# Second parts of the weight blocks: a negated rounding on ScalarE and an accumulating DMA in place of a subtraction on VectorE

## The chip, the core and the metric

The kernel runs on one core of a Trainium2 chip. The time is that of one execution in microseconds of the device; three runs of the kernel before gave 2616.05 to 2616.59, median 2616.26. The engines named below are TensorE (PE; its weight loads PEld), VectorE (DVE), ScalarE (ACT), GpSimd (POOL) and SyncE (SP), which here only issues loads and stores. Every engine works through its own list of instructions in order; semaphores tie the lists together.

## What is computed

The reference runs two layers over 512 latent tokens and 256 context tokens of 1024 features, all in float32. Each layer has a SwiGLU half-step, a mixer, and a second SwiGLU half-step, with norms that are scaled and shifted by vectors computed from c:

```python
def _swiglu(h, w1, w3, w2):
    return (jax.nn.silu(h @ w1) * (h @ w3)) @ w2

for l in range(DEPTH):
    x = x + 0.5 * mx[2] * _swiglu(_modulate(_rmsnorm(x, norm_g[l, 0]), mx[0], mx[1]), ...)
    hx = _modulate(_rmsnorm(x, norm_g[l, 1]), mx[3], mx[4])
    ox, oy = _mixer(hx, hy, w_in[l], w_out[l], ...)   # pooling, retention, convolution
    x = x + mx[5] * ox
    x = x + 0.5 * mx[8] * _swiglu(_modulate(_rmsnorm(x, norm_g[l, 2]), mx[6], mx[7]), ...)
return _rmsnorm(x, final_g)
```

The context tokens y take the same steps, but for the last ones of the second layer. The output is the latent stream.

## The kernel before

Features lie on the partitions, tokens along the rows: 256 of the context, 512 latent. A float32 product is made of three passes of the rounded type fp32r. Each operand is written as a first part (the value rounded to fp32r) and a second part (what the rounding left), and `mm3` (L153) multiplies first by first (L155), first by second (L156, weights' first part wh) and second by first (L157, weights' second part wl). `split` (L148) makes the parts: a cast on ScalarE (L150) and a subtraction on VectorE (L151). It serves weights and activations alike.

All weights of the products come as 348 blocks of 128 rows, 284 of 1024 columns (512 KB) and 64 of 640 (320 KB), in the order of use that `weight_order` (L489) lists. `weights` (L519) hands out the next block and prepares those after it: it loads the block into a buffer raw by SP's queue (L528), takes buffers wh and wl and splits. There are 6 buffers of raw, 4 each of wh and wl, and the blocks are prepared 3 ahead of their use (LOOKAHEAD; 0 in the first blocks, before `run` sets it). A buffer of wh or wl can be written when TensorE has used the block four before it for the last time; one of raw can be loaded when the split of the block six before it is done.

TensorE's products run in `products` (L535): over 8 tiles k of the features, and at each k over the outputs that are made together. Most of the time those are one or two blocks at a time. At some places four blocks are begun together, first for the context, then for the latent tokens: `convolution` (L752), `keys` (L708), `values` with four blocks along the features (through `project_tokens`, L623), and the first two tiles of a SwiGLU step (`ffn` L568, `up` L547).

Chains through several engines (norm, taps of the convolution, retention, the vectors of the modulation) are generators, which `poll` resumes when a count of TensorE's time passes their due time. The modulation's vectors need w_mod, loaded in tiles wm (L273 and L355, SP) and summed on VectorE into macc (L301, L303). In the start, `run` (L1056) makes the first norm: diag and rstd on TensorE, rstd copied by ScalarE (L1087), a row modrow copied by ScalarE (L283), then ht on VectorE (L474) and h on ScalarE and VectorE (L476, L478, L480). The first product (L155, up) needs the first h.

In the mixer of the first layer the stream x is not held: `load_x` (L206) reads its 12 tiles back from DRAM by SP's queue before the output projection, whose results VectorE adds to x (L1034). The retention's scores sc are masked on VectorE (L935), then used by TensorE for o (L953); ScalarE scales o to y (L967).

Of the kernel before, what the change touches and what calls it, by code (L numbers as in the profile page):

```python
# [9 lines left out]
F32 = mybir.dt.float32  # L10
F32R = mybir.dt.float32r
I32 = mybir.dt.int32
AF = mybir.ActivationFunctionType
# [19 lines left out]
# groups of tokens: stream, first token, number of tokens  # L33
# [3 lines left out]
LOOKAHEAD = 3  # L37


def per_block(n):  # L40
    """Tiles of the output features in a block of w2 for n tiles of hidden features."""
    return 2 if n * P * 2 <= 1024 else 1
# [3 lines left out]
# columns of the packed per-feature parameters  # L46
# [13 lines left out]
# columns of the constants that depend on shapes alone  # L60
# [11 lines left out]
def pad_cols(pad):  # L72
    """Where the two streams' tokens lie in a row with zeros on both sides of each."""
    return {CTX: pad, LAT: LC + 3 * pad}, NT + 4 * pad


class Kernel:
# [12 lines left out]
    # Chains that pass through several engines are generators: each part is emitted when TensorE has  # L90
    # been given enough other work, counted by self.clock in us, since the part before; a negative
    # delay counts from when the part before was due.
# [25 lines left out]
    def drain(self, *tasks):  # L118
        """Emits what is left of these chains."""
# [28 lines left out]
    def split(self, src, hi, lo):  # L148
        """src = hi + lo exactly, each part narrow enough for one pass of TensorE."""
        self.nc.scalar.copy(hi, src)  # L150
        self.nc.vector.tensor_sub(lo, src, hi.bitcast(F32))  # L151
# [8 lines left out]
    def rsqrt(self, src, n, scale, s):  # L160
        """(src * scale + EPS) ** -0.5 by Newton's steps from a guess by the exponent's bits."""
# [15 lines left out]
    def setup(self):  # L177
# [12 lines left out]
        # silu of both conditions: [P, KD, (ctx, lat)]  # L190
# [7 lines left out]
    def x_slots(self, st, n=LX):  # L198
        """The tiles of a stream and where they lie in its rows of DRAM."""
# [8 lines left out]
    def store_x(self, st):  # L208
        """Makes room while the mixer has no need of the stream."""
# [5 lines left out]
    def decays(self):  # L215
        """Per layer: the masks of decays within a chunk, and the weights by position."""
# [9 lines left out]
        # log1p(e) = 2 atanh(e / (2 + e))  # L226
# [11 lines left out]
        # weights of keys by position, and of a whole chunk: [P, l, dir, h]  # L238
# [37 lines left out]
    def mod_direct(self, l, j, half, raws):  # L276
        """Half of an adaLN vector straight on TensorE, where all engines wait for it."""
# [9 lines left out]
    def mod_halfway(self, l, j, half, raws):  # L287
        """The same with VectorE's multiplications."""
# [16 lines left out]
    def mod_fold(self, acc, rows):  # L305
        """Sums over each 32 partitions; what feature 32 b + i gives lies in column b on partition i."""
# [7 lines left out]
    def mod_sums(self, l, j, halves, rows):  # L314
        """The four sums of each feature together, and the bias: a feature per partition."""
# [16 lines left out]
    def mod_turn(self, row):  # L332
        """Two rows of 512 features to columns: [P, feature tile, condition]."""
# [12 lines left out]
    def mod_chunks(self, l, js, pace):  # L346
        """adaLN vectors in the background: VectorE multiplies, TensorE sums over partitions."""
# [15 lines left out]
    def scale(self, l, idx, st, dt):  # L363
        """Norm weight times 1 + scale for the idx-th sublayer."""
# [26 lines left out]
    def square(self, dt, grp, accs):  # L391
        """Adds the squares of a tile of x to the group's sum."""
# [10 lines left out]
    def mean_square(self, grp, accs):  # L403
        """Sums of squares, a token per partition: [P, tiles of tokens]."""
# [7 lines left out]
    def diag(self, r):  # L412
        """Diagonal matrices of 1 / rms."""
# [8 lines left out]
    def rstd(self, grp, dg):  # L422
        """The same on all partitions, in PSUM."""
# [8 lines left out]
    def put(self, tiles, p, k, grp, s):  # L432
        """part() of a tile that may not have a place yet."""
# [12 lines left out]
    def norm(self, l, idx, grp, accs, h):  # L446
        """Starts a group's norm; need() before its use."""
# [835 lines left out]
```

## Time and profile before

| | us |
|---|---|
| median of the runs | 2616.26 |
| span of the profiled execution | 2612.7 |
| TensorE busy (matmuls) | 2580.8 |
| VectorE busy | 1624.4 |
| ScalarE busy | 722.5 |
| GpSimd busy | 0.2 |

The profile shows one execution; its span runs from the first to the last instruction, so it is a little shorter than a run's time. Matmuls are pipelined, so the durations of neighbours overlap; the distance from one start to the next tells the pace. A view of waits names for each idle stretch of an engine the instruction that ended it. Windows give the busy time of each engine in a stretch of the span, with the clock that was granted to TensorE as a share of its full level (1.00 is 2.4 GHz, 0.50 is 1.2 GHz) and the share of time that the DMA engines were busy. For transfers, the time to landing counts from the issue to the completion.

### The profile page before, as it was taken

What the parts mean: (1) busy time and instruction counts of PE and PEld (TensorE: products, weight loads), DVE (VectorE), ACT (ScalarE), POOL (GpSimd) and SP (SyncE); (2) the same over time, 40 slices, a digit from 0 to 9 for tenths busy, and PEclk for the clock granted to TensorE, in tenths of its full rate; (3) what the DMA queues carried; (4) which work ended last, traced back from release to release, by engine and by line L of the source; (5) the groups of instructions that cost most, each with busy time, mean ns of one, the idle gap of its engine ahead of it and who ended that gap; (6) DMA issues with size and microseconds to landing.
All of it is one profiled execution on the core that took longest, in us unless ns stands there. A gap on an engine that the chain in (4) does not pass through costs nothing. (4 is left out here: it accounts for less than half of the span.)

```text
span 2612.7 us, 35462 instructions
## 1 busy us (share of the span) xinstructions
PE 2580.8 (99%) x14434; PEld 2241.5 (86%) x14434; DVE 1624.4 (62%) x3058; ACT 722.5 (28%) x1204; POOL 0.2 (0%) x4
## 2 busy tenths in 40 slices
PE   8999999999999999999999999999999999999998
PEld 4888888888898888888888888888888888888887
DVE  6776685747977777677333863645536697633335
ACT  3212112133334331212212412121223254422223
POOL 0000000000000000000000000000000000000000
PEclk9999999999999999999999999999999999999999
DMA  7343443322232134354211241433212332233331
GB/s 279 115 146 113 145 153 104 113 85 87 85 97 81 57 105 151 96 158 126 72 61 57 85 134 57 136 105 97 81 58 98 97 109 81 74 106 111 96 96 35
DMA packets 88003, 270.82 MB, mean 104 GB/s; under 512 B 10272, under 2 KB 12832, under 8 KB 87840
## 3 DMA queue, kind: packets, MB, share of 16 engines
q1 hardware_dynamic: 84768, 264.36, 32.1%
q10 hardware_dynamic: 3072, 4.20, 0.6%
q8 instruction: 113, 1.85, 0.3%
q14 instruction: 50, 0.41, 0.0%
HBM read 256.98 MB, written 7.34 MB: 101 GB/s over the span
## 5 line engine op out<-in xcount | busy, mean ns | idle before, releaser
L155 PE MATMUL up<-h,wh 128*128 128x512 f32 (+1 forms) x2496 | 852.1, 343 | 3.4 <-ACT h L476 1.7
L156 PE MATMUL up<-h,wh 128*128 128x512 f32 (+1 forms) x2496 | 853.0, 342 | 0.4 <-DVE h L478 0.2
L157 PE MATMUL up<-h,wl 128*128 128x512 f32 (+1 forms) x2496 | 849.9, 342 | 0.1
L150 ACT CAST wh<-raw 128x1024 fp32r<-128x1024 f32 (+1 forms) x348 | 344.0, 993 | 1261.7 <-PE down L156 442.2
L151 DVE TENSOR_TENSOR wl<-raw,wh 128x1024 fp32r<-128x1024 f32 (+1 forms) x348 | 398.2, 1148 | 333.1 <-ACT wh L150 318.2
L155 PEld LDWEIGHTS up<-h,wh 128*128 128x128 f32 x2496 | 472.2, 190 | 59.4 <-ACT h L476 2.0
L156 PEld LDWEIGHTS up<-h,wh 128*128 128x128 f32 x2496 | 473.0, 190 | 55.9 <-DVE h L478 1.0
L157 PEld LDWEIGHTS up<-h,wl 128*128 128x128 f32 x2496 | 472.3, 189 | 54.5 <-DVE wl L151 0.3
L155 PE MATMUL down<-g,wh 128*128 128x512 f32 (+1 forms) x1264 | 430.9, 341 | 0.0
L156 PE MATMUL down<-g,wh 128*128 128x512 f32 (+1 forms) x1264 | 430.3, 341 | 0.0
L157 PE MATMUL down<-g,wl 128*128 128x512 f32 (+1 forms) x1264 | 429.0, 339 | 0.0
L303 DVE SCALAR_TENSOR_TENSOR macc<-wm,sc,macc 128x512 f32<-128x512 f32 x462 | 319.0, 745 | 9.8 <-DMA wm<-in_w_mod_dram 9.6
L562 DVE TENSOR_TENSOR silu<-silu,up 128x512 f32<-128x512 f32 (+1 forms) x156 | 88.3, 566 | 341.1 <-PE up L157 340.7
L155 PEld LDWEIGHTS down<-g,wh 128*128 128x128 f32 x1264 | 239.7, 190 | 27.5 <-ACT g L150 0.2
L156 PEld LDWEIGHTS down<-g,wh 128*128 128x128 f32 x1264 | 239.8, 190 | 26.8 <-DVE g L151 0.6
L157 PEld LDWEIGHTS down<-g,wl 128*128 128x128 f32 x1264 | 239.3, 189 | 27.1
L599 DVE SCALAR_TENSOR_TENSOR x<-down,gate,x 128x256 f32<-128x256 f32 (+1 forms) x288 | 177.7, 621 | 136.3 <-PE down L157 134.4
L150 ACT CAST g<-silu 128x512 fp32r<-128x512 f32 (+1 forms) x156 | 81.8, 525 | 210.5 <-DVE silu L562 210.5
L745 DVE SCALAR_TENSOR_TENSOR conv<-z,dwh,conv 128x512 f32<-128x512 f32 (+1 forms) x180 | 109.8, 656 | 1.6
L151 DVE TENSOR_TENSOR g<-silu,g 128x512 fp32r<-128x512 f32 (+1 forms) x156 | 88.6, 568 | 23.7 <-ACT g L150 23.6
L561 ACT ACTIVATE silu<-up 128x512 f32<-128x512 f32 (+1 forms) x156 | 77.3, 496 | 87.0 <-PE up L157 86.7
L476 ACT ACTIVATE h<-ht,mod 128x256 fp32r<-128x256 f32 (+1 forms) x96 | 56.3, 597 | 81.5 <-DVE ht L474 81.4
(175 smaller groups left out, 2268.4 us busy)
## 6 DMA issues: line engine op xcount, KB each, us to landing
raw<-in_w_dram SPq DMA_DIRECT2D x224, 512.0 KB, 3.7
wm<-in_w_mod_dram SPq DMA_DIRECT2D x128, 512.0 KB, 3.9
raw<-in_w_dram SPq DMA_DIRECT2D x64, 320.0 KB, 3.0
raw<-in_w_feat_dram SPq DMA_DIRECT2D x36, 512.0 KB, 3.6
wm<-in_w_mod_dram SPq DMA_DIRECT2D x32, 256.0 KB, 6.0
raw<-in_w_out_dram SPq DMA_DIRECT2D x16, 512.0 KB, 4.8
xkept<-x SPq DMA_DIRECT2D x20, 256.0 KB, 2.5
x<-xkept SPq DMA_DIRECT2D x20, 256.0 KB, 6.0
```

What stands on the lines that cost most here:

```text
L150: self.nc.scalar.copy(hi, src)
L151: self.nc.vector.tensor_sub(lo, src, hi.bitcast(F32))
L155: nc.tensor.matmul(out, wh, xh, start=start, stop=False)
L156: nc.tensor.matmul(out, wh, xl, start=False, stop=False)
L157: nc.tensor.matmul(out, wl, xh, start=False, stop=stop)
L303: self.nc.vector.scalar_tensor_tensor(acc[v], raw, s, acc[v], op0=ALU.mult, op1=ALU.add)
L476: nc.scalar.activation(hi, t, AF.Identity, bias=sh)
L561: nc.scalar.activation(t, ps[f, 0], AF.Silu)
L562: nc.vector.tensor_mul(t, t, ps[f, 1])
L599: nc.vector.scalar_tensor_tensor(xd, ps, self.gate(l, idx, grp[0], dt), xd, op0=ALU.mult, op1=ALU.add)
L745: nc.vector.scalar_tensor_tensor(acc, src, w, acc, op0=ALU.mult, op1=ALU.add)
```

## The change

The second part of a weight block is made in another way. ScalarE casts the block into wh as before, and writes the block once more, times −1 and rounded by the same output type, into wl. Then GpSimd issues a DMA from raw to wl that adds what it carries to what lies there: wl = raw − rounded(raw). VectorE has no part in it. There are 5 buffers each of wh and wl and 4 of raw (the same bytes in all), and blocks are prepared 4 ahead. A raw buffer comes free when the accumulate that read it has landed. The rest of the diff takes away comments and texts, and moves line numbers behind L533 by two.

```diff
-LOOKAHEAD = 3
+LOOKAHEAD = 4
...
     def raw(self, n):
-        return self.wpool.tile([P, 1024], F32, tag="raw", name=self.name("raw"), bufs=6)[:, :n]
+        return self.wpool.tile([P, 1024], F32, tag="raw", name=self.name("raw"), bufs=4)[:, :n]
...
             raw = self.raw(n)
             self.nc.sync.dma_start(raw, src)
-            hi = self.wpool.tile([P, 1024], F32R, tag="wh", name=self.name("wh"), bufs=4)[:, :n]
-            lo = self.wpool.tile([P, 1024], F32R, tag="wl", name=self.name("wl"), bufs=4)[:, :n]
-            self.split(raw, hi, lo)
+            hi = self.wpool.tile([P, 1024], F32R, tag="wh", name=self.name("wh"), bufs=5)[:, :n]
+            lo = self.wpool.tile([P, 1024], F32R, tag="wl", name=self.name("wl"), bufs=5)[:, :n]
+            self.nc.scalar.copy(hi, raw)
+            self.nc.scalar.activation(lo, raw, AF.Copy, scale=-1.0)
+            self.nc.gpsimd.dma_start(lo, raw, accum_op=ALU.add)
             self.ahead.append((hi, lo))
```

The order on ScalarE in the start, before: four casts (the first two blocks pairs of the first SwiGLU step), then modrow, rstd and the first tiles of h.

```order
L150 CAST wh_103_347<-raw_102_345 128x1024 [waits DMAHW0_49]
L150 CAST wh_106_353<-raw_105_351 128x1024 [waits DMAHW1_49]
L283 COPY modrow_54_240<-modf_48_196 2x512 [waits PE_49]
L1087 COPY rstd_56_244<-rstd_55_242 128x256 [waits PE_49]
L1087 COPY rstd_58_248<-rstd_57_246 128x512 [waits PE_49]
L476 ACTIVATE h0_83_303<-ht_82_301,mod000_255 128x256 [waits DVE_49]
L476 ACTIVATE h0_83_303<-ht_85_306,mod000_255 128x256 [waits DVE_49]
L476 ACTIVATE h0_87_312<-ht_86_310,mod000_255 128x256 [waits DVE_49]
```

The same place after, from the fourth block's cast on; three pairs of cast and negation stand ahead of these rows.

```order
L531 CAST wh_106_356<-raw_105_354 128x1024 [waits DMAHW1_49]
L532 ACTIVATE wl_107_357<-raw_105_354 128x1024
L283 COPY modrow_54_240<-modf_48_196 2x512 [waits PE_49]
L1089 COPY rstd_56_244<-rstd_55_242 128x256 [waits PE_49]
L1089 COPY rstd_58_248<-rstd_57_246 128x512 [waits PE_49]
L531 CAST wh_109_363<-raw_108_361 128x1024 [waits DMAHW4_49]
L532 ACTIVATE wl_110_364<-raw_108_361 128x1024
L476 ACTIVATE h0_83_305<-ht_82_303,mod000_255 128x256 [waits DVE_49]
L476 ACTIVATE h0_83_305<-ht_85_308,mod000_255 128x256 [waits DVE_49]
```

Each cast is followed by its negation, and a fifth block's pair, which stood behind the tiles of h, stands ahead of the first of them.

The order on SP at the same time, before: loads of raw blocks, two of wm for later vectors, then those of wm0 (L273).

```order
L528 DMA raw_102_345<-in_w13_dram 128x1024 [waits DMAHW0_49]
L528 DMA raw_105_351<-in_w13_dram 128x1024 [waits DMAHW1_49]
L528 DMA raw_108_357<-in_w13_dram 128x1024 [waits DMAHW2_49]
L528 DMA raw_111_363<-in_w13_dram 128x1024 [waits DMAHW3_49]
L355 DMA wm_161_626<-in_w_mod_dram 128x1024 [waits DMAHW4_49]
L355 DMA wm_167_659<-in_w_mod_dram 128x1024 [waits DMAHW5_49]
L528 DMA raw_114_369<-in_w13_dram 128x1024 [waits DMAHW6_49,DVE_49]
L273 DMA wm0_66_269<-in_w_mod_dram 128x512 [waits DMAHW7_49]
```

And after; the names DMASW in a wait are the semaphores of GpSimd's transfers.

```order
L528 DMA raw_102_347<-in_w13_dram 128x1024 [waits DMAHW0_49]
L528 DMA raw_105_354<-in_w13_dram 128x1024 [waits DMAHW1_49]
L355 DMA wm_164_640<-in_w_mod_dram 128x1024 [waits DMAHW2_49]
L355 DMA wm_170_673<-in_w_mod_dram 128x1024 [waits DMAHW3_49]
L528 DMA raw_108_361<-in_w13_dram 128x1024 [waits DMAHW4_49,DMAHW6_49,DMASW0_49,Activation_49]
L528 DMA raw_111_368<-in_w13_dram 128x1024 [waits DMAHW5_49,DMAHW7_49,DMASW1_49,Activation_49]
L273 DMA wm0_66_271<-in_w_mod_dram 128x512
L273 DMA wm0_67_273<-in_w_mod_dram 128x512
```

The fifth and sixth loads of raw have moved behind the two wm, and wait for the transfers that read the first two raw buffers.

The order on TensorE where the keys of the first layer begin, before, up to the first product with the second block's second part (wl_810); the first row is the first product of the keys.

```order
L155 MATMUL kq_877_5630<-h0_766_5097,wh_806_5277 128x256 [waits Activation_49]
L156 MATMUL kq_877_5630<-h1_767_5098,wh_806_5277 128x256
L157 MATMUL kq_877_5630<-h0_766_5097,wl_807_5278 128x256 [waits DVE_49]
L155 MATMUL kq_878_5631<-h0_766_5097,wh_809_5283 128x256 [waits Activation_49]
L156 MATMUL kq_878_5631<-h1_767_5098,wh_809_5283 128x256
L155 MATMUL kq_877_5630<-h0_766_5097,wh_806_5277 128x256
L156 MATMUL kq_877_5630<-h1_767_5098,wh_806_5277 128x256
L155 MATMUL kq_879_5632<-h0_766_5097,wh_812_5289 128x256 [waits Activation_49]
L156 MATMUL kq_879_5632<-h1_767_5098,wh_812_5289 128x256
L157 MATMUL kq_877_5630<-h0_766_5097,wl_807_5278 128x256
L155 MATMUL kq_877_5630<-h0_770_5106,wh_806_5277 128x256
L157 MATMUL kq_878_5631<-h0_766_5097,wl_810_5284 128x256 [waits DVE_49]
```

And after, the last rows up to the same product; 17 matmuls of the keys stand between the convolution's last one and the first of these.

```order
L156 MATMUL kq_880_5720<-h1_778_5201,wh_806_5353 128x256
L157 MATMUL kq_880_5720<-h0_777_5200,wl_807_5354 128x256
L155 MATMUL kq_880_5720<-h0_777_5200,wh_806_5353 128x256
L156 MATMUL kq_880_5720<-h1_778_5201,wh_806_5353 128x256
L157 MATMUL kq_880_5720<-h0_777_5200,wl_807_5354 128x256
L155 MATMUL kq_880_5720<-h0_781_5210,wh_806_5353 128x256
L155 MATMUL kq_883_5723<-h0_769_5179,wh_815_5374 128x256 [waits DVE_49,Activation_49]
L156 MATMUL kq_883_5723<-h1_770_5180,wh_815_5374 128x256
L156 MATMUL kq_880_5720<-h1_782_5211,wh_806_5353 128x256
L157 MATMUL kq_880_5720<-h0_781_5210,wl_807_5354 128x256
L155 MATMUL kq_880_5720<-h0_781_5210,wh_806_5353 128x256
L157 MATMUL kq_881_5721<-h0_769_5179,wl_810_5361 128x256 [waits DMASW5_49]
```

The first product with wl_810 stands 28 matmuls behind the start of the keys, where it stood 11 behind it; products of the first block (kq_880) have moved ahead of it.

The order on SP where x is reloaded, before.

```order
L528 DMA raw_1123_7383<-in_w_out_dram 128x1024 [waits DMAHW0_49,DVE_49]
L528 DMA raw_1190_7873<-in_w_out_dram 128x1024 [waits DMAHW1_49,DVE_49]
L528 DMA raw_1193_7879<-in_w13_dram 128x1024 [waits DMAHW2_49,DVE_49]
L206 DMA x_1102_7341<-xkept_781_5137 128x512 [waits PE_49]
L206 DMA x_1103_7343<-xkept_781_5137 128x512 [waits PE_49]
```

And after: the raw load ahead of the loads of x waits for GpSimd's transfer.

```order
L528 DMA raw_1123_7483<-in_w_out_dram 128x1024 [waits DMAHW2_49,DMAHW6_49,DMASW0_49,Activation_49]
L528 DMA raw_1126_7490<-in_w_out_dram 128x1024 [waits DMAHW3_49,DMASW1_49,Activation_49]
L206 DMA x_1105_7445<-xkept_784_5219 128x512 [waits DVE_49,PE_49]
L206 DMA x_1106_7447<-xkept_784_5219 128x512 [waits DVE_49,PE_49]
L206 DMA x_1107_7449<-xkept_784_5219 128x512 [waits DVE_49]
```

The load of the raw block that stands just ahead of x waited for VectorE (DVE_49), and now for GpSimd's transfer (DMASW1_49).

## Rows read from the trace of the kernel before

**Rows 1.** Page: busy time by engine; then a DMA queue: packets, MB, share.

```profile
PE 2580.8 (99%) x14434; PEld 2241.5 (86%) x14434; DVE 1624.4 (62%) x3058; ACT 722.5 (28%) x1204; POOL 0.2 (0%) x4
...
q1 hardware_dynamic: 84768, 264.36, 32.1%
```

**Rows 2.** TensorE's waits: total us, times, longest us.

```profile
PE cb L862 <- ACT y L967: 1.9, 1, 1.9
...
PE o L953 <- DVE sc L935: 1.6, 2, 1.4
```

**Rows 3.** Windows: busy us by engine (count), granted clock, DMA share, GB/s.

```profile
0.00:60.00 60.00, 47.32 (x171) 22.07 (x171) 40.33 (x90) 21.90 (x38) 0.20 (x4) 0.97 0.82 303
60.00:750.00 690.00, 690.00 (x3951) 608.99 (x3951) 501.80 (x920) 174.97 (x286) 0.00 (x0) 1.00 0.36 112
750.00:850.00 100.00, 95.47 (x615) 84.27 (x614) 68.24 (x241) 46.83 (x114) 0.00 (x0) 0.98 0.29 95
```

**Rows 4.** Page, groups of the splits: total us, mean ns, idle before.

```profile
L150 ACT CAST wh<-raw 128x1024 fp32r<-128x1024 f32 (+1 forms) x348 | 344.0, 993 | 1261.7 <-PE down L156 442.2
L151 DVE TENSOR_TENSOR wl<-raw,wh 128x1024 fp32r<-128x1024 f32 (+1 forms) x348 | 398.2, 1148 | 333.1 <-ACT wh L150 318.2
```

**Rows 5.** Timeline of ScalarE, the start: start us, us, line, operation.

```profile
26.19 1.04 ACT L150 CAST wh<-raw 128x1024 fp32r<-128x1024 f32 x1 [5.60 <-DMA raw<-in_w_dram]
...
30.03 1.05 ACT L150 CAST wh<-raw 128x1024 fp32r<-128x1024 f32 x1 [0.23 <-DMA raw<-in_w_dram]
30.98 0.57 ACT L283 COPY modrow<-modf 2x512 f32<-2x512 f32 x1
31.46 1.03 ACT L1087 COPY rstd<-rstd 128x256 f32<-128x256 f32 x2
32.85 0.91 ACT L476 ACTIVATE h<-ht,mod 128x256 fp32r<-128x256 f32 x2 [0.36 <-DVE ht L474]
```

**Rows 6.** DMA issues: operation, count, KB each, median us to landing.

```profile
swap<-u ACTq DMA_DIRECT2D x64, 64.0 KB, 2.1
```

**Rows 7.** The raw loads' line, L528: landing.

```profile
DMA to landing us min/median/max: 2.8/3.7/9.0
```

**Rows 8.** Timeline of TensorE, the start: the first product.

```profile
33.41 0.50 PE L155 MATMUL up<-h,wh 128*128 128x256 f32 x2 [1.21 <-ACT h L476]
```

**Rows 9.** Windows of 1 us in the first mixer, columns as above.

```profile
795.00:796.00 1.00, 1.00 (x7) 1.00 (x6) 0.00 (x0) 1.00 (x5) 0.00 (x0) 0.50 0.46 168
798.00:799.00 1.00, 1.00 (x7) 0.91 (x6) 0.04 (x1) 1.00 (x4) 0.00 (x0) 0.82 0.00 0
817.00:818.00 1.00, 0.28 (x2) 0.00 (x0) 0.68 (x2) 0.00 (x0) 0.00 (x0) 1.00 1.06 408
```

**Rows 10.** Timeline where the keys begin: TensorE and ScalarE.

```profile
629.67 0.39 PE L157 MATMUL cv<-h,wl 128*128 128x512 f32 x1
...
629.87 2.95 ACT L150 CAST wh<-raw 128x1024 fp32r<-128x1024 f32 x3 [11.47 <-PE cv L156]
629.90 0.39 PE L155 MATMUL cv<-h,wh 128*128 128x512 f32 x1
...
631.94 0.28 PE L155 MATMUL kq<-h,wh 128*128 128x256 f32 x1
...
632.05 0.28 PE L156 MATMUL kq<-h,wh 128*128 128x256 f32 x1
```

**Rows 11.** Timeline at the reload of x, several engines; then its landing, L206.

```profile
804.98 1.22 DVE L151 TENSOR_TENSOR wl<-raw,wh 128x1024 fp32r<-128x1024 f32 x1 [0.76 <-ACT wh L150]
...
806.61 8.14 SPq L206 DMA_DIRECT2D x<-xkept  x12
...
817.32 0.75 DVE L1034 SCALAR_TENSOR_TENSOR x<-mo,mod,x 128x512 f32<-128x512 f32 x1 [3.97 <-PE mo L157]
...
818.73 0.49 PE L953 MATMUL o<-v,sc 128*128 128x128 f32 x2 [1.44 <-DVE sc L935]
...
DMA to landing us min/median/max: 4.3/5.8/6.8
```

## What the change does to the time: the prediction

> **What bounds the kernel now.** I read the busy line of the page first: TensorE's matmuls take 2580.8 of 2612.7 us, VectorE 1624.4, ScalarE 722.5, GpSimd 0.2 [rows 1]. So the end is set by TensorE, and an edit on another engine moves the time only where TensorE waits. The list of what TensorE waited for comes second; past the very start its longest are ScalarE's y (1.9 us) and VectorE's sc (1.6) [rows 2]. No line of that list names the weight blocks' second parts; the splits are early enough everywhere. The windows by stage show where the missing 32 us are: 12.7 in the first 60 us and 4.5 between 750 and 850, while 60 to 750 is full to the last tenth [rows 3]. The rest lies in the second layer's mixer and the tail. What can be won from a free VectorE is therefore some 5 to 10 us, and what can be lost is whatever delay reaches a matmul.
>
> The profiled execution's span is 2612.7 us and the median of the runs 2616.26, 3.6 more; I work on the span and add the same 3.6.
>
> **What the change removes and adds.** 348 subtractions leave VectorE (398.2 us busy), and 348 negative copies come to ScalarE; their nearest row is the cast of the same block, 344.0 us in all and 1.04 us for a block of 1024 columns [rows 4, 5]. ScalarE goes to about 1066 us of 2613: still not the bound as a sum. GpSimd issues 348 accumulating transfers of 320 or 512 KB between two places of SBUF. None is in this trace. Four casts in the start are released 1.28 us apart by the landings of 512 KB blocks, so 1.28 us is what such a block costs all the DMA engines in a stream [rows 5]. If the accumulate reads two operands, it costs twice that: 284 × 2.56 + 64 × 1.6 = 829 us of all engines, 32% of the span on top of the loads' 32.1% [rows 1]. Together 64%: hidden on average.
>
> **How long one accumulate takes (L)**, from issue to landing, is the unknown of this case. Below it: a 64 KB transfer between two places of SBUF lands after 2.1 us [rows 6]. Above it: the slowest raw block took 9.0 us. The nearest row is the median raw block, of the same 512 KB, 3.7 us [rows 7]; the second read adds another 1.28. I take L = 5.0 and keep 2.1 and 9.0 for the range.
>
> The Trainium skill ("DMA: Bandwidth & Descriptors", Anatomy of one DMA) gives 2.0 us plus bytes over 436 GB/s for a GpSimd-issued transfer, 3.2 us for 512 KB; "Collectives: The Full Stack" (Why ReduceScatter is half of AllGather) says that an add in flight is not slow by itself but reads two sources and so runs at half the rate, which makes it 4.4 us, an estimate from these two pages. No row here shows either. By 4.4 in place of 5.0 the sum below would be some 6 us smaller.
>
> **Term 1, the start.** In the new order ScalarE has a fifth cast with its negation ahead of the first h, and that block's load on SP waits until block 0's accumulate has landed, because raw has four buffers. Before: casts at 26.19 to 30.03, modrow 30.98, rstd 31.46, first h 32.85, TensorE's first product 33.41 [rows 5, 8]. After: four casts and four negations in a row end at 26.19 + 8 × 1.05 = 34.6; modrow and the two rstd (1.6 us) end at 36.2; a fifth pair at 38.3. That is the floor, 5.5 us later than 32.85, whatever L is. With L: block 0 is negated at 28.3, its accumulate lands at 33.3, or 34.6 with the loads still queued there (one more 1.28); raw of block 4 is issued, lands 3.7 later at 38.3, and its pair ends at 40.4: first h 7.5 us late. Small waits of TensorE just behind it (some 0.5 us) are absorbed. Term: +7.0, with +5.0 and +11 for L = 2.1 and 9.0. VectorE loses two subtractions before its macc chain there, so that chain isn't the next thing to be late.
>
> A gap costs a second time. Where TensorE waited 1.9 us for y before 794.0, the granted clock fell to 0.50 (1.2 GHz) by 795 and rose again at 798.4; after the 1.4 us before 818.7 it stayed at 1.00 [rows 2, 9]. Some 3.4 us at half are 1.7 us lost. The start's new gap of 9 us should bring one such stretch: +1.7.
>
> **Term 2, places where four blocks are begun at once** (convolution to keys, keys to values, and the first blocks of a SwiGLU step). Until TensorE's last product with an old block, ScalarE can't write the new one's buffers. In the row, casts of three blocks start as soon as the convolution's last products end, and the keys' first product follows 2 us later [rows 10]. With five buffers, the first of the four is already there. For the second, the new order of TensorE has 37 matmuls between the old block's last and the new second part's first: 9 of 512 columns and 28 of 256, which at the rows' spacing (0.23 and 0.11 to 0.12) is 5.2 to 5.4 us. Of 5.4, cast and negation need 2.1, so the accumulate must land in 3.3. Counted alike through the program, five places have 5.4 or 5.5 us, five more about 6.8 (4.7 left for L); the steady parts have over 13. Stalls: 5 × (5.0 − 3.3) + 5 × (5.0 − 4.7) = +10.0. With L = 3.7 it is 2, below 3.3 nothing, with 9.0 it is 28.5 + 21.5 = 50. At 1.7 us each these gaps are near the one that left the clock alone, so no clock term.
>
> **Term 3, x in the first layer's mixer.** Twelve loads of x stand on SP behind one raw block. Before, that block waited for a VectorE subtraction that ended at 806.2; the loads went out from 806.61, 0.68 apart, and land after 5.8 us [rows 11]. Now it waits for an accumulate: 806 + 5 = 811, 4.8 later. The fifth load's x is read by VectorE's L1034 at 817.32; it had landed near 809.3 + 5.8 = 815.1, so 2.2 us of the delay are slack and 2.6 go through. Behind L1034 on VectorE stands sc, and TensorE waits for that already [rows 2, 11]. Term: +2.6 (0 to +7), and the gap grows from 1.4 to 4.0 us, so a half-clock stretch comes with it: +1.7.
>
> **Term 4, what VectorE gives back.** Between 785 and 800 TensorE waited for ScalarE's y [rows 2], and on ScalarE a cast stands between two y's. In the new order cast and negation stand ahead of both and their buffers are free earlier, so the wait and its half-clock stretch can shrink; but a negation is added on the engine that is late. −2.0, from −5 to +4.
>
> **Sum.** 7.0 + 1.7 + 10.0 + 2.6 + 1.7 − 2.0 = +21.0 us: span 2633.7, time 2616.3 + 21.0 = 2637.3, say **2637 us**, 0.8% slower.
>
> **Rivals.** (a) Short accumulates, L of 3.3 or less: terms 2 and 3 nearly vanish, the floor of the start stays: 5.0 + 1.7 + 1 − 2 = +6, 2622. For it: swap's 2.1 us [rows 6]. Against it: eight times the bytes. Chance 0.22. (b) Long accumulates, over 6 and up to 9 us, because loads, modulation weights and accumulates share the engines: 11 + 50 + 7 + some five clock stretches (8) − 2 = +74 at 9, 2690. For it: the loads' own 9.0 [rows 7] and a DMA share of 1.06 where loads stand together, as at 817 [rows 9]; against: the 64% mean. If the queue carried only one at a time, L over 5 would also set the pace of the last SwiGLU step, and the time leave the range. Chance 0.18. (c) Faster: if the fifth pair doesn't hold back the first h and the accumulates land in under 3.3 us, terms 1 to 3 are nothing, and a lighter VectorE and the moved cast clear the mixers: 4.5 us between 750 and 850 [rows 3], as much in the second layer, and a clock stretch of 1.7, about −10: 2606. It decides at the start: it holds only if the first h comes before 34. The order on ScalarE and four negations of 1.04 us speak against it. Chance 0.06. (d) All of it hidden, TensorE's 99% unmoved: 2616. It needs the same start. Chance 0.04.
>
> **How the numbers follow.** My forecast, L between 3.4 and 6, has 0.50 and gives 2624 to 2655 by the same terms. The range takes in (a) and most of (b), and leaves out (c), half of (d) and the tail: 2618 to 2690. About 0.2%, 5.2 us, is what a measurement of this kernel can tell from no change. Faster by that: 0.06. Within: (d) and half of (a), 0.15. Slower: 0.79.
>
> **What would show it.** Term 1: ScalarE's first h at about 40 instead of 32.85, waiting for a raw load. Term 2: TensorE waits of 1 to 2 us named after the accumulate's queue, in the keys and where SwiGLU steps begin. Term 3: a longer wait for sc near 840. L itself: the accumulate's row among the transfers. It is wrong if the first h comes by 35, if L is under 3.3 or over 7, or if a wait appears in the steady parts.

## The result: slower by 2.9%, and the profile after

The changed kernel takes 2692.59 us in the median (2690.31 to 2694.36) against 2616.16; the ratio is 1.0294, 95% interval 1.0281 to 1.0306. The forecast was 2637 with 2618 to 2690: the sign was right, the size was off by 55 us of 76, and the time fell just beyond the range.

The page of the changed kernel, engines and DMA queues, beside [rows 1]; q0 is the queue of GpSimd's transfers:

```profile
span 2692.5 us, 36376 instructions
...
PE 2603.4 (97%) x14434; PEld 2259.5 (84%) x14434; DVE 1253.2 (47%) x2710; ACT 1023.4 (38%) x1552; POOL 299.8 (11%) x352
...
q0 software_dynamic: 50112, 169.89, 34.3%
q1 hardware_dynamic: 84768, 264.36, 29.4%
```

VectorE lost 371 us and ScalarE gained 301, while the span grew by 80. The transfers take 34.3% of the 16 engines, by the prediction's reckoning 32%. TensorE's waits, beside [rows 2] (total us, times, longest):

```profile
PE up L155 <- ACT h L476: 12.1, 2, 11.6
PE up L157 <- DMA wl<-raw: 11.8, 6, 2.7
PE cv L157 <- DMA wl<-raw: 10.2, 4, 4.8
...
PE kv L903 <- ACT vw L897: 7.8, 1, 7.8
PE o L955 <- DVE sc L937: 6.3, 1, 6.3
PE kq L157 <- DMA wl<-raw: 6.3, 4, 2.9
PE down L155 <- ACT g L150: 4.4, 1, 4.4
PE g L157 <- DMA wl<-raw: 3.9, 1, 3.9
```

Here the waits for the accumulating transfers stand by name: up, cv, kq and g, 32 us in all, where before no wait for a second part was seen. Around them stand waits that were not there or short before: the first h (12.1), vw (7.8, before 0.9), sc (6.3, before 1.6 in two waits), g of a SwiGLU step (4.4).

The landing times: medians by operation, then the shortest, median and longest of all the transfers of line L533, beside [rows 6, 7].

```profile
wl<-raw POOLq DMA_DIRECT2D x284, 512.0 KB, 5.5
raw<-in_w_dram SPq DMA_DIRECT2D x224, 512.0 KB, 4.4
```

```profile
DMA to landing us min/median/max: 3.6/5.5/11.8
```

From the starts of the matmuls (the distance to the next start, less the usual distance for the shape) TensorE's lost time can be placed: 46 us before, 125 after. Of the 79 between them, waits longer than 0.3 us make 62 (25 before, 87 after) and matmuls at half clock 21 (3 before, 24 after); the rest is 5 less than before. By place: the start 13; where four blocks begin together 38; the first mixer behind 750 13; a stall at 379 in the first SwiGLU step 6; the second mixer 8. These sums are good to some 2 us.

### The profile page after: what moved, and what is told of

It is laid out like the page before. It is cut to its first block, busy times and chain, and to the rows that moved or that the text cites. A ratio compares the mean times of both kernels' runs of the same rounds, so it can differ in the third digit from the quotient of the medians.

```text
span 2692.5 us, 36376 instructions
## 1 busy us (share of the span) xinstructions
PE 2603.4 (97%) x14434; PEld 2259.5 (84%) x14434; DVE 1253.2 (47%) x2710; ACT 1023.4 (38%) x1552; POOL 299.8 (11%) x352
## 3 DMA queue, kind: packets, MB, share of 16 engines
q0 software_dynamic: 50112, 169.89, 34.3%
## 5 line engine op out<-in xcount | busy, mean ns | idle before, releaser
L155 PE MATMUL up<-h,wh 128*128 128x512 f32 (+1 forms) x2496 | 855.6, 344 | 12.2 <-ACT h L476 12.1
L157 PE MATMUL up<-h,wl 128*128 128x512 f32 (+1 forms) x2496 | 855.3, 343 | 11.8 <-DMA wl<-raw 11.8
L533 POOL DMA_DIRECT2D wl<-raw x348 | 299.6, 861 | 2352.5 <-ACT wl L532 2202.5
L532 ACT ACTIVATE wl<-raw 128x1024 fp32r<-128x1024 f32 (+1 forms) x348 | 346.0, 994 | 27.7 <-issue 12.2
L563 ACT ACTIVATE silu<-up 128x512 f32<-128x512 f32 (+1 forms) x156 | 76.3, 490 | 41.2 <-PE up L157 41.2
```

The lines of the kernel that those rows point to most:

```text
L155: nc.tensor.matmul(out, wh, xh, start=start, stop=False)
L157: nc.tensor.matmul(out, wl, xh, start=False, stop=stop)
L532: self.nc.scalar.activation(lo, raw, AF.Copy, scale=-1.0)
L533: self.nc.gpsimd.dma_start(lo, raw, accum_op=ALU.add)
```

## Experiments

Three explanations stood against each other. A: the transfers' landing times, stretched where several transfers and loads share the DMA engines. B: ScalarE's second pass over each block. C: two raw buffers fewer, which hold the loads back.

### Which part of the change costs the time

**e1_buffers.** The kernel before with the change's counts of buffers.

```diff
-LOOKAHEAD = 3
+LOOKAHEAD = 4
...
-        return self.wpool.tile([P, 1024], F32, tag="raw", name=self.name("raw"), bufs=6)[:, :n]
+        return self.wpool.tile([P, 1024], F32, tag="raw", name=self.name("raw"), bufs=4)[:, :n]
...
-            hi = self.wpool.tile([P, 1024], F32R, tag="wh", name=self.name("wh"), bufs=4)[:, :n]
-            lo = self.wpool.tile([P, 1024], F32R, tag="wl", name=self.name("wl"), bufs=4)[:, :n]
+            hi = self.wpool.tile([P, 1024], F32R, tag="wh", name=self.name("wh"), bufs=5)[:, :n]
+            lo = self.wpool.tile([P, 1024], F32R, tag="wl", name=self.name("wl"), bufs=5)[:, :n]
```

> The kernel before with the new counts of buffers alone (raw 4, wh and wl 5 each, four blocks ahead); VectorE still subtracts. Theory A (the added transfer's time to landing, stretched where several of them and loads share the DMA engines): 2612 to 2628, the start a few us later since a fifth block's cast may stand ahead of the first h. Theory C (four raw buffers in place of six hold the loads back): most of the 76 us, 2660 or more. Theory B (ScalarE's second pass over each block): 2616.

Measured 2620.99, ratio 1.0019 (1.0010 to 1.0029): +5.3 us. C is out as the main cause.

**e2_no_add.** The changed kernel without the transfer.

```diff
-            self.nc.gpsimd.dma_start(lo, raw, accum_op=ALU.add)
```

> The changed kernel without the accumulating transfer: wl holds minus the rounded block, so the second part of the weights is left wrong; casts, negations, buffers and four blocks ahead as in the change. A: 2618 to 2634, the start's floor of 5 us with its half-clock stretch and some us for a busier ScalarE. B: 2670 or more. C: 2660 or more.

2623.18, ratio 1.0029 (1.0018 to 1.0040): +7.5, so the negations add 2.2 to the buffers' 5.3, and the two intervals overlap. B alone is out. Two waits are longer than in e1, vw of the second mixer (5.1 us) and modrow (2.8).

**e4_plain_copy.** The transfer writes the same bytes, but doesn't add.

```diff
-            self.nc.gpsimd.dma_start(lo, raw, accum_op=ALU.add)
+            self.nc.gpsimd.dma_start(lo.bitcast(F32), raw)
```

> The changed kernel with a plain transfer from raw to wl by the same queue in place of the accumulating one, so that wl holds the raw block (the second part of the weights is left wrong); same bytes written, one read fewer. A, with the share of the DMA engines that the second read takes as the main thing: 2635 to 2665, a landing of about 4 us and half the DMA share of 34% for this queue. A, with the fixed part of a GpSimd transfer as the main thing: 2675 to 2695. B or C: no different from the change, 2692.

2646.72, ratio 1.0120 (1.0105 to 1.0135): +31.0. The page and the line of the plain copy:

```profile
PE 2589.4 (98%) x14434; PEld 2249.2 (85%) x14434; DVE 1254.8 (47%) x2710; ACT 1024.8 (39%) x1552; POOL 184.8 (7%) x352
...
q0 software_dynamic: 46016, 169.89, 16.3%
```

```profile
DMA to landing us min/median/max: 2.4/3.4/8.1
```

Added in this order, of the 76.4 us the buffers are 5.3, the negations 2.2, a plain transfer 23.5 and the adding 45.4. In another order the parts would differ: e3 and e7 below show the buffers and the negation at other prices beside the transfers. The queue's share goes from 16.3% to 34.3%, a factor of 2.1 for the same bytes written; the shortest landing from 2.4 to 3.6 us, the median from 3.4 to 5.5.

**e5_half_add.** Accumulate half the columns.

```diff
-            self.nc.gpsimd.dma_start(lo, raw, accum_op=ALU.add)
+            self.nc.gpsimd.dma_start(lo[:, : n // 2], raw[:, : n // 2], accum_op=ALU.add)
```

> The changed kernel with an accumulating transfer of the first half of each block's columns alone (the other half of the second part is left wrong): half the bytes, two reads. If the cost goes by the reads of the DMA engines (theory A), its queue takes about 17% of 16 engines, as the plain copy's 16.3% did, single landings near 3 us, and the time is 2640 to 2660, as the plain copy's 2646.7. If an accumulating transfer has a fixed price of its own (theory D), landings stay near 5 and the time 2670 or more.

2654.41, ratio 1.0149 (1.0134 to 1.0164): 8 us over the plain copy of twice the bytes.

```profile
q0 software_dynamic: 50112, 84.96, 18.8%
...
wl<-raw POOLq DMA_DIRECT2D x284, 256.0 KB, 3.6
```

Half the bytes with two reads take nearly the engines' time of all the bytes with one (18.8% and 16.3%), and nearly the same time in the end. So the cost goes with what the transfers take of the DMA engines; at most the 8 us between the two are left for a fixed price of the accumulating form.

**e3_old_buffers.** The changed kernel with 6 raw, 4 of wh and wl, three ahead (e1's diff the other way round).

> The changed kernel with the counts of before (raw 6, wh and wl 4 each, three blocks ahead): the accumulating transfer stays. A: worse than the change, 2720 to 2800, since at each place where four blocks begin one more block waits for cast, negation and transfer. C: 2616 to 2650, the loads being free again.

2722.96, ratio 1.0411 (1.0394 to 1.0429). The change's counts, the fifth buffer of wh and wl with its fourth block ahead above all by A's account, are worth 30 us to the transfers, though they cost 5 without them. The three counts were not changed one by one.

### Where it costs

**e8_mixed.** VectorE's subtraction for 83 chosen blocks, the transfer for 265 (the expectation's 84 and 264 are miscounted by one, e13's 247 too). The other runs of this part differ in the list alone:

```diff
+            self.made = getattr(self, "made", -1) + 1
+            if any(a <= self.made < b for a, b in ((0, 6), (72, 109), (176, 181), (248, 283))):
+                self.split(raw, hi, lo)
+            else:
                 self.nc.scalar.copy(hi, raw)
                 self.nc.scalar.activation(lo, raw, AF.Copy, scale=-1.0)
                 self.nc.gpsimd.dma_start(lo, raw, accum_op=ALU.add)
```

> The changed kernel, but VectorE's subtraction for 84 of the 348 blocks: the first 6, those of the two mixers with the blocks about them, and those where a SwiGLU step begins; the other 264 take the negation and the accumulating transfer. A: the transfers cost nothing where blocks come one at a time, so 2618 to 2632: the counts of buffers cost 5 (measured) and the stall in the modulation's sums near 380 may stay (6). If the transfers cost by the piece everywhere, 264/348 of the 69 us stay: 2670 to 2678.

2629.37, ratio 1.0053 (1.0036 to 1.0070): 76% of the transfers stay and 82% of the loss is gone.

**e11_mixed_old.** The same with the buffers of before.

> The mixed kernel (VectorE's subtraction for 84 blocks, negation and accumulating transfer for 264) with the counts of buffers of before: raw 6, wh and wl 4, three blocks ahead. If the buffers explain 5 of its 13 us: 2620 to 2626, the start as before and the stall in the modulation's sums near 375 left. If transfers need the fifth buffer even where blocks come one at a time: 2640 or more.

2623.40, ratio 1.0027 (1.0016 to 1.0038): 6 us less than e8, as e1 had cost 5. One large wait was left:

```profile
PE down L155 <- ACT g L150: 4.1, 1, 4.1
```

**e13_no_sums.** The list of e11 with (36, 53) added: 17 more blocks by VectorE, those in use between 300 and 420 us.

> The mixed kernel with the buffers of before, and VectorE's subtraction for 17 more blocks, those used while the sums of the modulation wait for their tiles between 300 and 420 us (101 blocks by VectorE, 247 by the transfer). If the one stall left there (7.6 us with its half-clock stretch) comes from transfers that share the DMA engines with the modulation's tiles: 2614 to 2618, no different from before. If it comes from the order of the work on VectorE, or the transfers cost a little everywhere: 2621 to 2625.

2615.90, ratio 1.0000 (0.9991 to 1.0009). The wait for g is no longer in the list, and 248 accumulating transfers cost nothing that can be measured. They gain nothing either, though VectorE works 262 us less than before; TensorE's longest waits are those of before (y 1.9, sc 1.4):

```profile
PE 2582.5 (99%) x14434; PEld 2244.1 (86%) x14434; DVE 1362.7 (52%) x2810; ACT 932.9 (36%) x1452; POOL 214.5 (8%) x252
```

**e15_bursts.** The change with VectorE's subtraction where four blocks begin: the list is ((74, 84), (104, 109), (176, 181), (248, 257), (276, 283)).

> The changed kernel with VectorE's subtraction for the 36 blocks that are begun four at a time or stand just behind such a place (convolution, keys and values of both layers, first tiles of three SwiGLU steps). By the gaps of the changed kernel's trace and their half-clock stretches these places hold some 40 of the 78 us: 2648 to 2660. If the cost lies in the mixers' chains behind them (x, the gates, vw): 2670 or more.

2647.67, ratio 1.0124 (1.0107 to 1.0141): 36 blocks in 348 hold 45 us of the 76. No wait for wl is left in TensorE's list. By the matmuls' distances some 39 us of this come back at the places themselves and 7 in the first mixer, where the wait for wl before g (3.9 us) goes with them.

**e14_start.** The list is ((0, 6),).

> The changed kernel with VectorE's subtraction for the first 6 blocks alone. The start then takes what it takes with the buffers alone (excess 18 in place of 26): 2682 to 2686. If a fifth pair ahead of the first h and not the transfers holds the start up: 2690 or more.

2689.22 (2682.29 to 2690.15), ratio 1.0276 (1.0261 to 1.0292). The wait for the first h falls from 12.1 to 4.8 us, and the lost time of the first 100 us from 27 to 21; in the runs' times 3 us of this are seen, and the intervals overlap. The time lies between the two expectations: the transfers did hold up the start, but part of what it gave back is lost further on (the waits for wl in kq grow from 6.3 to 7.6 us).

### Mechanisms

**e7_neg_dve.** The negation on VectorE.

```diff
-            self.nc.scalar.activation(lo, raw, AF.Copy, scale=-1.0)
+            self.nc.vector.tensor_scalar(lo, raw, -1.0, None, op0=ALU.mult)
```

> The changed kernel with the negation on VectorE instead of ScalarE; the transfer stays. A: 2680 to 2695, ScalarE's queue being a small part (2 us between the runs with buffers alone and without the transfer). Theory B (ScalarE's second pass in its list delays what stands behind it, vw of the second mixer above all): 2650 to 2675. A rival from the Trainium skill (SBUF — State Buffer, Who interferes with whom): VectorE's fast modes keep GpSimd from writing its descriptors; then landings get longer and the time is 2700 or more.

2670.59, ratio 1.0213 (1.0198 to 1.0228): 22 us less than the change, in B's range rather than A's. The negation costs 2 us without transfers and 22 with them: on VectorE it takes 652 ns and runs beside the next cast, so that each transfer of a row of blocks goes out earlier (0.7 us apart in the keys, 1.9 in the change). By the trace this is about half of the gain: where four blocks begin, the waits for wl fall from 28 to 22 us and half clock from 10 to 5. Most of the rest lies where TensorE waits behind ScalarE: vw falls from 7.8 to 2.1 us, g from 4.4 to 1.7. So beside the transfers ScalarE's second pass does cost, as B says. The start lost as much as in the change, with waits for wl in place of the wait for h. The median landing is 5.4 us as in the change (the longest is 15.5), so the rule of the Trainium skill that the expectation names, by which landings would get longer, is not seen at work here.

**e10_neg_first.** Negation ahead of the cast on ScalarE (the two lines exchanged).

> The changed kernel with the negation ahead of the cast on ScalarE for each block: the transfer can go out 1.05 us earlier, the first part comes 1.05 us later. A (a stall where blocks are begun together is negation, cast and landing added up, against the time that TensorE's order leaves): some ten places gain about 1 us each and some lose their half-clock stretch, 2672 to 2686. If the stalls are set by the sharing of the DMA engines alone, all transfers only move together and the gain is under 4 us: 2688 to 2694.

2687.55, ratio 1.0272 (1.0256 to 1.0287): 5 us less, between the two expectations, the interval touching that of the change. Moving every transfer by one microsecond helps little when the next block's transfer still waits for two passes; in e7 shortening the row helped.

**e9_x_queue.** The reload of x on GpSimd's queue.

```diff
-            self.nc.sync.dma_start(self.x[st][i], src[:, c])
+            (queue or self.nc.sync).dma_start(self.x[st][i], src[:, c])
...
-            self.load_x(st, self.kept[st])
+            self.load_x(st, self.kept[st], nc.gpsimd)
```

> The changed kernel with the reload of x issued by GpSimd's queue instead of SP's, so that it no longer stands behind a raw load that waits for a landing. If term 3 is that order on SP: x comes some 4 us earlier in the first mixer, TensorE's wait for sc falls from 6.3 to 1.4 to 3 us and the half-clock stretch behind it may go: 2680 to 2688. If it is the sharing of the DMA engines: no change, 2690 to 2695.

2692.25, ratio 1.0296 (1.0280 to 1.0311), no different in time. But the wait itself did what term 3 says:

```profile
PE o L955 <- DVE sc L937: 1.8, 1, 1.8
```

It fell from 6.3 to 1.8 us, so the order on SP was its cause. The gain doesn't show in the median; the profiled spans differ by 3 us (2689.6 and 2692.5), less than the four runs differ among each other (2690.55 to 2696.08). By the matmuls' distances the first mixer loses 5 us less and the SwiGLU step behind it 2 more; why that step loses more stays open.

**e6_pool_sub** and **e12_pool_mixers** looked for a version ahead of both kernels: GpSimd subtracts itself, for all blocks (with the change's buffers) or for 46 blocks inside the mixers (with those of before). The edit of e6; e12 has the same line in place of `self.split` for blocks 81 to 104 and 255 to 276:

```diff
-            self.nc.scalar.activation(lo, raw, AF.Copy, scale=-1.0)
-            self.nc.gpsimd.dma_start(lo, raw, accum_op=ALU.add)
+            self.nc.gpsimd.tensor_sub(lo, raw, hi.bitcast(F32))
```

> The changed kernel with the second part made by a subtraction on GpSimd (from the block and its cast) instead of negation and transfer; buffers and four blocks ahead as in the change. It takes the transfer's traffic off the DMA engines and the negation off ScalarE. A: GpSimd's subtraction takes some 2 to 3 us in place of 1.05 + 4.5 to 12, so 2620 to 2640. If GpSimd works beside VectorE at less than half its pace, 4 us and over a block, 2650 or more.

2690.94, ratio 1.0287 (1.0272 to 1.0303).

> The kernel before with GpSimd's own subtraction instead of VectorE's for the 46 blocks inside the two mixers, no transfers and the buffers of before. If a lighter VectorE shortens the mixers' waits (term 4), 2608 to 2614 and the first version ahead of both; if GpSimd's subtraction is slower than the slack of a block, or the waits hang on ScalarE, 2616 to 2630.

2651.34, ratio 1.0131 (1.0114 to 1.0148). Both lost. In e6 a block takes the 2 to 3 us of the first expectation, but the time is 50 us over it: TensorE waits 32 us for VectorE's parts of the norm (acc and diag, before 6) and 13 for GpSimd's wl. In e12 the largest wait is one of 14.9 us for wl in the second layer's keys. GpSimd's subtraction there took 36.7 us (the median of the 46 is 2.4), while VectorE ran 60 two-operand sums of the convolution without a gap, and ended 2 us behind them; e6 has one such, 35.3 us long. VectorE's row and the subtraction in e12:

```profile
2091.87 39.84 DVE L750 SCALAR_TENSOR_TENSOR conv<-z,dwh,conv 128x512 f32<-128x512 f32 x60
```

```profile
L534 POOL TENSOR_TENSOR wl<-raw,wh x1: 36726/36726/36726, 2097.2 to 2097.2; 128x1024 fp32r<-128x1024 f32 x1
```

Groups of e6, in which GpSimd makes all subtractions (busy us, mean ns):

```profile
L532 POOL TENSOR_TENSOR wl<-raw,wh 128x1024 fp32r<-128x1024 f32 (+1 forms) x348 | 836.3, 2408 | 1816.5 <-ACT wh L531 1785.9
...
L303 DVE SCALAR_TENSOR_TENSOR macc<-wm,sc,macc 128x512 f32<-128x512 f32 x462 | 405.7, 931 | 13.4 <-DMA wm<-in_w_mod_dram 13.0
```

```profile
L151 DVE TENSOR_TENSOR g<-silu,g 128x512 fp32r<-128x512 f32 (+1 forms) x156 | 194.8, 1249 | 79.0 <-ACT g L150 78.9
```

GpSimd needs 2408 ns for a block in the mean, VectorE 1148 [rows 4]; and some of VectorE's own work grows beside it, a split of g from 572 ns in the change to 1249, a sum of macc from 747 to 931, while silu (L563) stays at 565.

## Why the prediction was wrong

**The bound and the sign** held: TensorE was full, a lighter VectorE bought nothing (262 us less in e13: 1.0000), and nearly all of the loss came as waits of TensorE and half clock behind them.

**L was right, its use was not.** The median landing is 5.5 us against 5.0 taken. But term 2 used this one value for each place where four blocks begin, and there the transfers share the engines with each other and with loads. In the keys of the first layer, ScalarE and GpSimd of the changed kernel (start, us, line, what the wait ended on):

```profile
655.33 1.05 ACT L531 CAST wh<-raw 128x1024 fp32r<-128x1024 f32 x1 [11.47 <-PE cv L156]
...
656.28 1.06 ACT L532 ACTIVATE wl<-raw 128x1024 fp32r<-128x1024 f32 x1
...
657.24 1.03 ACT L531 CAST wh<-raw 128x1024 fp32r<-128x1024 f32 x1
...
657.63 0.86 POOL L533 DMA_DIRECT2D wl<-raw  x1 [37.76 <-ACT wl L532]
...
659.52 0.86 POOL L533 DMA_DIRECT2D wl<-raw  x1 [1.03 <-ACT wl L532]
...
661.42 0.86 POOL L533 DMA_DIRECT2D wl<-raw  x1 [1.04 <-ACT wl L532]
```

Shortest, median and longest landing of the four transfers issued from 655 to 666:

```profile
DMA to landing us min/median/max: 4.5/7.1/11.8
```

And the products that waited for them:

```profile
662.20 0.38 PE L157 MATMUL kq<-h,wl 128*128 128x256 f32 x1 [1.10 <-DMA wl<-raw]
...
665.09 0.39 PE L157 MATMUL kq<-h,wl 128*128 128x256 f32 x1 [0.72 <-DMA wl<-raw]
...
670.12 0.58 PE L157 MATMUL kq<-h,wl 128*128 128x256 f32 x1 [2.85 <-DMA wl<-raw]
```

The cast at 655.33 starts as the convolution's last products end, as in [rows 10], and cast and negation take the 2.1 us that the prediction gave them. The transfers go out at 657.6, 659.5, 661.4 and 664.3 and land after 4.5, 5.5, 8.7 and 11.8 us. Meanwhile the DMA engines are full (share 1.03, second from the right), while TensorE nearly stands still at 667 to 669:

```profile
659.00:661.00 2.00, 2.00 (x18) 1.90 (x16) 0.00 (x0) 2.00 (x3) 0.86 (x1) 1.00 1.03 199
...
667.00:669.00 2.00, 0.27 (x3) 0.07 (x1) 2.00 (x5) 0.00 (x0) 0.00 (x0) 1.00 1.03 213
```

From the page, a block of 512 KB takes 2.85 us of all engines (34.3% of 2692.5 us, over 284 blocks and 64 of five eighths, 324 in all). Sent 1.9 us apart, the transfers come faster than that, and from 662 on loads stand among them. The first three landings end the three waits of 1.1, 0.7 and 2.9 us; nothing waits for the fourth. In the second layer's convolution a row of three gives the same picture, here its landings and its longest wait:

```profile
DMA to landing us min/median/max: 4.6/5.5/10.5
```

```profile
2115.76 0.80 PE L157 MATMUL cv<-h,wl 128*128 128x512 f32 x1 [4.80 <-DMA wl<-raw]
```

The step that failed is term 2's "5 × (5.0 − 3.3) + 5 × (5.0 − 4.7)", with one L for every place and no clock: it measured 38 by the trace in place of 10. The times that it allowed for a landing were right: at the nine places where TensorE waited, the landing less the first wait is 3.2 to 3.5 or 4.5 to 4.8 us, for the forecast's 3.3 and 4.7. But the landings waited for took 4.5 to 8.5 us there, and these nine waits came to 17 us; five more waits behind them in the same rows, for landings of up to 10.5, added 11; and half clock took 10. The 64% mean share hid that what counts here is the share of a few microseconds.

**The start** has the same fault. ScalarE in the changed kernel, beside [rows 5]:

```profile
32.78 1.05 ACT L532 ACTIVATE wl<-raw 128x1024 fp32r<-128x1024 f32 x1
33.73 0.56 ACT L283 COPY modrow<-modf 2x512 f32<-2x512 f32 x1
34.20 0.83 ACT L1089 COPY rstd<-rstd 128x256 f32<-128x256 f32 x2
43.87 1.04 ACT L531 CAST wh<-raw 128x1024 fp32r<-128x1024 f32 x1 [8.83 <-DMA raw<-in_w_dram]
...
45.77 0.90 ACT L476 ACTIVATE h<-ht,mod 128x256 fp32r<-128x256 f32 x2
```

Landings of the four transfers issued from 28 to 36, and of the one raw load issued there:

```profile
DMA to landing us min/median/max: 6.4/7.4/9.8
```

```profile
DMA to landing us min/median/max: 8.9/8.9/8.9
```

The four casts and negations ended at 33.8, where the prediction had 34.6 (they start 0.95 us apart and not 1.05). Block 0's transfer went out at 28.5 and took the shortest of these, 6.4 us, to 34.9, also near the forecast's 34.6. Then "raw of block 4 is issued, lands 3.7 later" failed: it took 8.9 us (34.9 to 43.8), with the transfers of blocks 1 to 3 on the engines beside it, and from 37.4 on the next raw block and tiles wm0. The window of the first 60 us has a DMA share of 1.00, before 0.82 [rows 3]:

```profile
0.00:60.00 60.00, 36.92 (x116) 17.95 (x117) 25.96 (x64) 25.31 (x40) 4.67 (x9) 0.80 1.00 328
```

The first h came at 45.8, forecast 40.4, before 32.85. The term measured 13 by the trace (with its half-clock stretch) against 8.7.

**x in the first mixer.** The mechanism is as told (e9). The wait grew by 5 us rather than 2.6: the fifth load of x took 9.0 us to land, with a transfer of wl among the loads, where the median before was 5.8 [rows 11]. The clock was the larger miss: two windows of 2 us behind that wait (granted clock third from the right).

```profile
862.00:864.00 2.00, 1.83 (x6) 1.50 (x6) 2.00 (x5) 0.00 (x0) 0.00 (x0) 0.50 1.06 395
870.00:872.00 2.00, 2.00 (x14) 2.00 (x13) 0.62 (x4) 0.00 (x0) 0.00 (x0) 0.68 0.00 0
```

It was still below full at 870, 8 us after the wait had ended, and cost 5.2 us instead of 1.7.

**The clock** as a term: two stretches were forecast (3.4 us); by the matmuls' distances it cost some 21 us more than before. At the places of term 2 the six waits of 2.5 to 4.8 us came with half clock, and those of 1.7 us and less did not, as in the rows; the waits were longer than forecast, so the term was missing. But the length of a wait doesn't decide by itself: in the first mixer of e13 the wait for sc is 1.4 us, as before, and the clock behind it fell to half for some 7 us, where it had stayed full. The same window of the kernel before and of e13:

```profile
822.00:824.00 2.00, 1.67 (x8) 0.91 (x7) 2.00 (x5) 0.00 (x0) 0.00 (x0) 1.00 0.04 8
```

```profile
822.00:824.00 2.00, 2.00 (x7) 1.71 (x8) 2.00 (x4) 0.00 (x0) 0.00 (x0) 0.50 0.00 0
```

What decides there stays open.

**What no term named.** In the first SwiGLU step VectorE's sums of the modulation waited for tiles wm; silu stands behind them on VectorE, and TensorE waited 4.4 us for g (6 with the clock):

```profile
379.33 2.74 DVE L303 SCALAR_TENSOR_TENSOR macc<-wm,sc,macc 128x512 f32<-128x512 f32 x4 [1.25 <-DMA wm<-in_w_mod_dram]
381.98 0.68 DVE L564 TENSOR_TENSOR silu<-silu,up 128x512 f32<-128x512 f32 x1
```

e13 shows the cause: without transfers in that stretch the wait is gone. In the second mixer ScalarE's list has three casts with their negations ahead of the vw that TensorE needs, and two of these casts wait for raw loads:

```profile
2216.98 1.05 ACT L531 CAST wh<-raw 128x1024 fp32r<-128x1024 f32 x1 [2.65 <-DMA raw<-in_w_out_dram]
...
2220.83 1.04 ACT L531 CAST wh<-raw 128x1024 fp32r<-128x1024 f32 x1 [1.85 <-DMA raw<-in_w_out_dram]
...
2224.63 2.14 ACT L897 ACTIVATE vw<-v,wk 128x128 f32<-128x128 f32 x7
```

The pools take raw buffers too, and there are two fewer; that this is why the loads come late is argued, not shown. That wait is 1.8 us with the buffers alone, 5.1 with the negations, 7.8 in the change, 2.1 with the negation on VectorE, and 3.9 with the transfers and the buffers of before (e3). Term 4's own wait, for y in the first mixer, did shrink (from 1.9 us to 1.0 at the longest, without half clock behind it); the second mixer, which no term has, lost 8.

**The two rules.** The Trainium skill, "Collectives: The Full Stack" (Why ReduceScatter is half of AllGather) says that an add in flight reads two sources and runs at half the rate: the trace agrees, 34.3% of the engines against the plain copy's 16.3%. The Trainium skill, "DMA: Bandwidth & Descriptors" (Anatomy of one DMA), gives 3.2 us for 512 KB; the plain copies landed in 2.4 to 8.1, median 3.4. The estimate of 4.4 from both lies inside the 3.6 to 5.5 from shortest to median landing: the price of one transfer by itself was not what failed.

**Rival (b)** came nearest: long landings because loads, modulation and transfers share the engines, 2690. It had a chance of 0.18. Its reason was right and its L was not: the median of 5.5 lies in the forecast's own 3.4 to 6, so that its time came so close is partly luck. Its argument against, the 64% mean, should have been read in the stretches where four blocks begin, and in the start, where the profile before already showed a share of 0.82.

## What to carry to other kernels

Before moving work from an idle-enough engine to the DMA engines, look at the places where several blocks are asked for at once: here the transfers shared full engines, and the landings that TensorE waited for (up to 10.5 us) counted, not the median (5.5). Work taken off an engine that nobody waits for was worth nothing (262 us of VectorE, ratio 1.0000). Price a new wait of TensorE with the half-clock stretch that can follow it.

## What the runs showed of the hardware

- An accumulating transfer between two places of SBUF took 2.1 times the DMA engines' time of a plain one (34.3% and 16.3% of the span for 170 MB written), and GpSimd 861 ns per issue against 530 (299.6 and 184.6 us for 348).
- GpSimd's own subtraction of a block took 2408 ns in the mean beside a busy VectorE, and some of VectorE's two-operand work took up to 2.2 times longer beside it (a split of g 572 to 1249 ns; silu 567 to 565). Beside 60 such sums of VectorE in a row one subtraction of GpSimd took 36.7 us.
- After the wait of 6.3 us for sc, with thin work behind it, TensorE's clock stayed at 0.50 for some 10 us (861 to 871), against 3.4 us behind the wait of 1.9 us in the kernel before; behind the same wait of 1.4 us it fell in e13 and not in the kernel before.
